# Sums over later keys in stick-breaking attention: one full-precision product and a running block replaced by two products of operand parts, with the steps of attention placed anew

## The chip, the cores and the metric

The kernel runs on one core of a Trainium2 chip. The metric is the device time of one execution in microseconds (us). Five engines matter: TensorE (PE in the profile; its weight loads are PEld), VectorE (DVE), ScalarE (ACT), GpSimd (POOL), and SyncE (SP), which issues most DMAs. Each runs its own queue of instructions in order and waits on semaphores.

## What is computed

One decoder layer on 512 tokens of width 2048, all in float32. The part that the change touches is the attention, with 8 heads of 128:

```python
z = jnp.einsum('bhqd,bhkd->bhqk', qi, kf).astype(jnp.float32) * scale
strict = key_pos[None, :] < q_pos[:, None]
log_beta = jax.nn.log_sigmoid(z)
log_1m = jnp.where(strict, jax.nn.log_sigmoid(-z), jnp.zeros_like(z))
tail = lax.cumsum(log_1m, axis=3, reverse=True) - log_1m
w = jnp.where(strict, jnp.exp(log_beta + tail), jnp.zeros_like(z))
return jnp.einsum('bhqk,bhkd->bhqd', w.astype(vf.dtype), vf)
```

For each query, `tail` at a key is the sum of `log_1m` over the later keys. Around it stand the projections `u, v_sgu, q, k, v_att, g_a, g_b = h @ W_in`, a spatial gating, the merge with `w_up_a`, `w_up_b` and `w_o`, a SwiGLU block (`w_ffn_in`, `w_ffn_out`) and a gate with per-layer embeddings (`w_gate`, `w_ple`).

## The kernel before

Activations lie transposed: 128 features on the partitions and the 512 tokens along the free axis. All large products are made from operand parts: a float32 operand is rounded by ScalarE into a high part of type float32r (L266 for activations, L334 for weights) and VectorE subtracts that from the operand for the low part (L267, L331). Three products, high by high, high by low and low by high, are summed in PSUM (`mm3`, L271 to L273). Most of them run in Strassen's form, seven products of 256 columns for a pair of 256 by 256 blocks; some are plain, with 512 columns. `Pair` (L572) makes two 128-row output tiles at once; `Pair.mix` (L645) puts the seven products together on ScalarE and VectorE, in a tile `o` that is either a home given by the caller or one of the two 128 by 1024 tiles of the pool tag `out` (`wide`).

Weights arrive through four landing buffers. SP loads them (L314, L316, L318), POOL issues a DMA that adds one block of the weights onto another as it lands (L338), ScalarE and VectorE split them into one of three slots. The order of the work is made in Python: `tick` counts units of the large products, and what has been put off with `after` or `beside` is written at its tick, between two units. A step that yields `n` goes on `n` ticks later. In the stage here a tick is one unit, 21 products of 256 columns.

The input projection goes in four rounds. A round makes q, k and v of two heads (one `Pair` each) and then three or four gate tiles; the attention of these two heads runs beside the following pairs (loop at L1195, order at L1124). Its steps, before the change:

- `q_prep` (L970) normalises q in place in the block `y_b[rnd]`, which is also q's home; `k_prep`, `v_prep` likewise. `flip` (L942, products at L946) transposes through PSUM.
- `stage_a` (L1002): one product of keys and queries in float32 (L1007) into a small PSUM bank (pool of two, also used by `flip`), four passes of ScalarE (L1009 to L1014), two of VectorE (L1016, L1018: `w`, the log of beta, and `zs`, minus `log_1m`) and POOL's mask of the diagonal block (L1020).
- `stage_b` (L1025): the sums over later keys. `tri` by `zs` in float32 (L1030) sums within the block of 128 keys, `ones` by `later` (L1032) adds the later blocks. `later` holds the sum of the later blocks' `zs`, kept by POOL (L1040) and VectorE (L1042). Then VectorE subtracts (L1034), ScalarE takes the exponential (L1044) and POOL masks (L1045).
- `finish` (L1050): four float32 products with v (L1054), a copy (L1056), and for the second head the store to DRAM (L1058).

A head has four key blocks, j = 3 to 0, with 128, 256, 384 and 512 query columns. The attention begins 5 ticks after v is made.

All of SBUF's working memory is two arenas, `parts` (float32r) and `wholes` (float32), in which blocks are taken and given while the program is written; `place` asks for a start at a multiple of `PLACE`. The size of the arenas and the places taken decide which earlier reader a DMA must wait for. `fits` decides at which tick an operand is built.

Of the kernel before, what the change touches and what calls it, by code (L numbers as in the profile page):

```python
# [12 lines left out]
F32 = mybir.dt.float32  # L13
F32R = mybir.dt.float32r
AF = mybir.ActivationFunctionType
ALU = mybir.AluOpType
# [21 lines left out]
PARTS = 16 * PLACE  # L38
WHOLES = 13824
# [26 lines left out]
def hybrid_layer(  # L66
# [44 lines left out]
    class Arena:  # L111
# [5 lines left out]
        def take(self, n, how="low"):  # L117
# [359 lines left out]
    def load(src, n=1024):  # L477
        b = take(n, "old")
        nc.sync.dma_start(out=b.f(0, 1024), in_=src)
        return b  # L480
# [91 lines left out]
    class Pair:  # L572
# [72 lines left out]
        def mix(self, o):  # L645
# [3 lines left out]
            s = tmp.tile([P, T], F32, tag="p75", name=nm("p75"), bufs=1)  # L649
            s7, s5 = s[:, :256], s[:, 256:]  # L650
# [24 lines left out]
        def mix_doubled(self, o):  # L675
# [4 lines left out]
            s5 = tmp.tile([P, T], F32, tag="p75", name=nm("p75"), bufs=1)[:, :256]  # L680
# [140 lines left out]
    def load_x():  # L821
# [109 lines left out]
    def a_tiles():  # L931

        for tag, n in (("l", T), ("later", 3 * P), ("w0", T), ("w1", 3 * P), ("w2", 2 * P), ("w3", P),
                       ("k", 1024), ("v", 1024), ("zs", 1024)):
            att[tag] = take(n)

# [33 lines left out]
    def q_prep(o):  # L970

        for h in range(2):
            yield 2
            s = o[:, h * T : (h + 1) * T]
            ps = flip(s)
# [7 lines left out]
            nc.scalar.activation(s, flip(q.f()), AF.Copy, scale=gcol[:, g_q : g_q + 1])  # L983
# [13 lines left out]
    def attention(rnd, qT, kT, rk, v):  # L997
        state = {}
        yield 1
        turn = [0]  # L1000

        def stage_a(h, j):  # L1002
# [5 lines left out]
            l = a_tile("l")[:, :n]  # L1008
            nc.scalar.activation(l, z, AF.Abs, scale=r)  # L1009
            turn[0] ^= 1  # L1010
            zs = a_tile("zs", n, turn[0] * T)
            nc.scalar.activation(zs, z, AF.Copy, scale=r)
            nc.scalar.activation(l, l, AF.Exp, scale=-1.0)
            nc.scalar.activation(l, l, AF.Ln, bias=1.0)  # L1014
            w = a_tile(f"w{j}", n)
            nc.vector.scalar_tensor_tensor(out=w, in0=zs, scalar=0.0, in1=l,  # L1016
                                           op0=ALU.min, op1=ALU.subtract)
            nc.vector.scalar_tensor_tensor(out=zs, in0=zs, scalar=0.0, in1=l,  # L1018
                                           op0=ALU.max, op1=ALU.add)
            nc.gpsimd.affine_select(out=zs[:, :P], in_=zs[:, :P], pattern=[[1, P]],  # L1020
                                    compare_op=ALU.is_gt, fill=0.0, base=0,
                                    channel_multiplier=-1)
            state[h, j] = zs, w

        def stage_b(h, j):  # L1025
# [4 lines left out]
            nc.tensor.matmul(tp, tri, sp, start=True, stop=j == NT - 1)  # L1030
            if j < NT - 1:
                nc.tensor.matmul(tp[:, P:], ones, later[:, j * P :], start=False,  # L1032
                                 stop=True)
            nc.vector.tensor_tensor(out=w, in0=w, in1=tp, op=ALU.subtract)  # L1034
            if j == NT - 1:
                later = a_tile("later", 3 * P)
                state[h, "later"] = later
            if j > 0:
                c = j * P
                nc.gpsimd.tensor_copy(later[:, c - P : c], sp[:, :P])  # L1040
# [21 lines left out]
        for h in range(2):  # L1062
            stage_a(h, 3)
            yield 2
            stage_a(h, 2)
            yield 1
            stage_b(h, 3)
            yield 1
            stage_a(h, 1)
            yield 1  # L1070
            stage_b(h, 2)
            yield 1
            stage_a(h, 0)
            yield 1
            stage_b(h, 1)
# [383 lines left out]
```

## Time and profile before

| what | us |
|---|---|
| time, median of 3 runs | 2718.68 |
| lowest and highest | 2717.98, 2721.21 |
| the profiled execution, its own time | 2719.95 |
| its span (first to last instruction) | 2718.3 |
| PE busy | 2693.0 |
| DVE busy | 2075.1 |
| ACT busy | 1353.5 |
| POOL busy | 449.2 |

Busy time of PE is modelled at the ends of instructions, so starts of neighbouring products say more than durations: the distance from one start to the next is what a product costs in a full queue. [...]

### The profile page before, as it was taken

The numbers are of one execution on the slowest core, as the hardware profiler recorded it, in microseconds if no ns is written. First come the engines' busy times: TensorE is split into PE (matmuls) and PEld (weight loads), VectorE is DVE, ScalarE is ACT, GpSimd is POOL, SyncE is SP. The second block draws the span as 40 slices with busy tenths as digits, with TensorE's granted clock in tenths as the row PEclk, the third lists the DMA queues.
The fourth block names the chain that finished last, engine by engine and source line by source line (L and its number), as shares of the span: only waits on it lengthen the run. The fifth ranks groups of instructions, "written<-read, shape, count | busy, mean of one in ns | idle before, by whom it ended". The sixth has DMA issues, their size and how long they took to land.

```text
span 2718.3 us, 45582 instructions
## 1 busy us (share of the span) xinstructions
PE 2693.0 (99%) x17243; PEld 2438.9 (90%) x17243; DVE 2075.1 (76%) x3377; ACT 1353.5 (50%) x2045; POOL 449.2 (17%) x527
## 2 busy tenths in 40 slices
PE   9999999999999999999999999999999999999999
PEld 7899999999999889988888888888888999989898
DVE  8566767667777667678889898989899567788876
ACT  7645556565554334365444444444445344453543
POOL 0222322232320000001111111111111111111110
PEclk9999999999999999999999999999999999999999
DMA  7567676767776447768888888887877669778784
GB/s 227 153 180 176 170 175 172 176 175 185 173 193 195 140 138 227 201 192 200 219 208 203 201 205 201 203 203 202 204 196 225 174 168 258 197 242 239 240 232 117
DMA packets 303132, 529.03 MB, mean 195 GB/s; under 512 B 25664, under 2 KB 162880, under 8 KB 302912
## 3 DMA queue, kind: packets, MB, share of 16 engines
q1 hardware_dynamic: 242160, 425.70, 49.0%
q0 software_dynamic: 60752, 100.43, 23.6%
q8 instruction: 135, 2.21, 0.3%
q14 instruction: 85, 0.70, 0.1%
HBM read 478.84 MB, written 47.19 MB: 194 GB/s over the span
## 4 chain that ended last, share of the span: by engine, by line
PE 95%; DMA 2%; DVE 1%; ACT 1%; issue 1%; POOL 0%; SPq 0%; ACTq 0%; DVEq 0%; POOLq 0%
PE ps L628 26%; PE ps L272 20%; PE ps L271 20%; PE ps L273 20%; PE small L628 4%; PE small L1054 1%; PE small L946 1%; PE small L1030 1%; PE small L1007 1%; DMA wholes<-x 0%; PE small L1032 0%; DMA ple<-out 0%; DVE wlo L331 0%; ACT whi L334 0%; PE small L1108 0%
## 5 line engine op out<-in xcount | busy, mean ns | idle before, releaser
L271 PE MATMUL ps<-parts,whi 128*128 128x256 f32 (+1 forms) x3995 | 1247.1, 314 | 13.3 <-ACT parts L266 7.4
L334 ACT ACTIVATE whi<-wholes 128x512 fp32r<-128x512 f32 (+4 forms) x950 | 856.1, 917 | 793.6 <-PE ps L272 305.3
L272 PE MATMUL ps<-parts,whi 128*128 128x256 f32 (+1 forms) x3960 | 1231.9, 311 | 1.3 <-DVE parts L267 1.3
L273 PE MATMUL ps<-parts,wlo 128*128 128x256 f32 (+1 forms) x3960 | 1230.4, 311 | 0.3 <-DVE wlo L331 0.3
L331 DVE TENSOR_TENSOR wlo<-wholes,whi 128x512 fp32r<-128x512 f32 (+4 forms) x950 | 964.9, 1050 | 156.5 <-ACT whi L334 155.0
L271 PEld LDWEIGHTS ps<-parts,whi 128*128 128x128 f32 x3995 | 764.2, 191 | 62.1 <-ACT parts L266 7.6
L272 PEld LDWEIGHTS ps<-parts,whi 128*128 128x128 f32 x3960 | 758.0, 191 | 44.7 <-DVE parts L267 2.2
L273 PEld LDWEIGHTS ps<-parts,wlo 128*128 128x128 f32 x3960 | 757.6, 191 | 38.9 <-DVE wlo L331 0.8
L628 PE MATMUL ps<-parts,whi 128*128 128x512 f32 x2064 | 683.2, 396 | 0.0
L628 PEld LDWEIGHTS ps<-parts,wlo 128*128 128x128 f32 x2064 | 387.9, 188 | 89.6
L628 PE MATMUL ps<-parts,wlo 128*128 128x256 f32 x2064 | 406.4, 278 | 0.0
L350 DVE TENSOR_TENSOR wholes<-wholes 128x256 f32<-128x256 f32 (+1 forms) x794 | 329.6, 415 | 27.5 <-issue 4.3
L628 PEld LDWEIGHTS ps<-parts,whi 128*128 128x128 f32 x2064 | 330.0, 189 | 2.1
L338 POOL DMA_DIRECT2D wholes<-w_ffn_in x172 | 149.7, 870 | 688.9 <-DVE wholes L350 229.7
L338 POOL DMA_DIRECT2D wholes<-w_in x132 | 118.8, 903 | 510.4 <-DMA wholes<-w_in 222.5
L687 DVE TENSOR_TENSOR out<-out,ps 128x256 f32<-128x256 f32 x258 | 107.6, 417 | 83.1 <-ACT out L684 83.0
L656 DVE TENSOR_TENSOR out<-out 128x256 f32<-128x256 f32 x59 | 25.0, 425 | 173.1 <-ACT out L653 172.8
L628 PE MATMUL small<-parts,whi 128*128 128x512 f32 x344 | 136.6, 397 | 0.0
L267 DVE TENSOR_TENSOR parts<-wholes,parts 128x1024 fp32r<-128x1024 f32 (+4 forms) x131 | 123.7, 953 | 14.0 <-ACT parts L266 13.5
L266 ACT ACTIVATE parts<-wholes 128x1024 fp32r<-128x1024 f32 (+4 forms) x131 | 105.7, 834 | 39.6 <-DVE wholes L497 15.6
L338 POOL DMA_DIRECT2D wholes<-w_ffn_out x56 | 57.0, 1031 | 401.0 <-DMA wholes<-w_ffn_out 187.5
L1299 ACT ACTIVATE out<-out 128x512 f32<-128x512 f32 x44 | 27.8, 633 | 161.2 <-DVE out L1298 161.2
(119 smaller groups left out, 1645.1 us busy)
## 6 DMA issues: line engine op xcount, KB each, us to landing
wholes<-w_ffn_in SPq DMA_DIRECT2D x172, 384.0 KB, 5.4
wholes<-w_in SPq DMA_DIRECT2D x132, 384.0 KB, 4.7
wholes<-w_ffn_in SPq DMA_DIRECT2D x172, 256.0 KB, 4.7
wholes<-w_ffn_in POOLq DMA_DIRECT2D x172, 256.0 KB, 5.2
wholes<-w_in SPq DMA_DIRECT2D x132, 256.0 KB, 3.8
wholes<-w_in POOLq DMA_DIRECT2D x132, 256.0 KB, 4.8
wholes<-x SPq DMA_DIRECT2D x32, 512.0 KB, 5.6
wholes<-w_ffn_out SPq DMA_DIRECT2D x31, 512.0 KB, 4.5
```

What stands on the lines that cost most here:

```text
L266: return (nc.scalar.activation(hi, src, AF.Copy), nc.vector.tensor_tensor(out=lo, in0=src, in1=hi.bitcast(F32), op=ALU.subtract))
L267: nc.vector.tensor_tensor(out=lo, in0=src, in1=hi.bitcast(F32), op=ALU.subtract))
L271: nc.tensor.matmul(ps[:, s], sh, mh[:, s], start=start, stop=False)
L272: nc.tensor.matmul(ps, sh, ml, start=False, stop=False)
L273: return nc.tensor.matmul(ps, sl, mh, start=False, stop=stop)
L331: in_turn(nc.vector.tensor_tensor(out=self.lo[:, blocks], in0=r, in1=h.bitcast(F32), op=ALU.subtract))
L334: in_turn(nc.scalar.activation(h, r, AF.Copy))
L338: nc.gpsimd.dma_start(out=raw[:, 3:5], in_=self.src[:, 1:3], accum_op=ALU.add)
L350: in_turn(nc.vector.tensor_tensor(out=o, in0=x, in1=y, op=ALU.add))
L628: m = nc.tensor.matmul(out, l, r, start=first and k == 0, stop=last and k == 1)
L687: in_turn(nc.vector.tensor_tensor(out=out, in0=x, in1=y, op=op))
L1299: nc.scalar.activation(g, g, AF.Silu)
```

## The change

The sum over later keys becomes two products of operand parts with one stationary matrix. `stage_b` now copies `zs` on ScalarE into its high part `zh`, `stage_c` makes the low part `zl` on VectorE, and `stage_d` multiplies `tri` by both in float32r. What the later blocks add comes in through row 0 of the operand: row 0 of a block's `zs` is not used by the sum within the block, so `tris[1]` has ones in row 0, and row 0 of the next block's `zs` is set to the sum of all keys of the later blocks (row 0 of the product plus the saved row 0, `first`). The running block `later`, its copies and additions, and the product with `ones` go. The former `stage_a` is cut in two: `stage_m` holds its VectorE and POOL part. The attention begins 6 ticks after k, with v made beside it, and a block takes three ticks.

Besides: q is made in an `out` tile and `y_b` is taken when q's first half is ready; `mix` works within `o` with three additions of 256 columns where it had one of 256 and one of 512; the arena `parts` grows by 1024 columns (for `zh` and `zl`) and `wholes` shrinks by 512; `place` starts at multiples of twice `PLACE`; the loads of the gate tiles take the lowest free place.

```diff
-PARTS = 16 * PLACE
-WHOLES = 13824
+PARTS = 16 * PLACE + 1024
+WHOLES = 13312
...
-                    start = -(-start // PLACE) * PLACE
+                    start = -(-start // (2 * PLACE)) * 2 * PLACE
...
-            copy(s, "q")
-            tt(b[:, 2], b[:, 1], s7)
-            tt(b[:, 1:4:2], b[:, 1:3], s5.unsqueeze(1).to_broadcast([P, 2, 256]))
+            copy(o[:, T:], "q")
+            tt(b[:, 2], b[:, 1], b[:, 2])
+            tt(b[:, 1], b[:, 1], b[:, 3])
+            tt(b[:, 3], b[:, 2], b[:, 3])
...
-    tri = consts.tile([P, P], F32, name="tri")
+    tris = [consts.tile([P, P], F32R, name=f"tri{i}") for i in range(2)]
+    tri = tmp.tile([P, P], F32, tag="diag", name="tri")
     nc.gpsimd.affine_select(out=tri, in_=ones, pattern=[[-1, P]], compare_op=ALU.is_gt,
                             fill=0.0, base=0, channel_multiplier=1)
+    nc.vector.tensor_copy(tris[0], tri)
+    nc.vector.memset(tri[0:1, :], 1.0)
+    nc.vector.tensor_copy(tris[1], tri)
...
+        def stage_m(h, j):
...
+            if j < NT - 1:
+                if j:
+                    nc.gpsimd.tensor_copy(first(j), s[0:1])
+                nc.gpsimd.memset(s[0:1, :P], 0.0)
+
+        def stage_b(j):
+            nc.scalar.activation(zh[:, : (NT - j) * P], sums(j), AF.Copy)
+
+        def stage_c(j):
             n = (NT - j) * P
-            sp, w = state.pop((h, j))
-            later = state.get((h, "later"))
-            tp = small_bank()[:, :n]
-            nc.tensor.matmul(tp, tri, sp, start=True, stop=j == NT - 1)
-            if j < NT - 1:
-                nc.tensor.matmul(tp[:, P:], ones, later[:, j * P :], start=False,
-                                 stop=True)
+            in_turn(nc.vector.tensor_tensor(out=zl[:, :n], in0=sums(j), in1=att["zh"].f(0, n),
+                                            op=ALU.subtract))
+
+        def stage_d(h, j):
+            n, w = (NT - j) * P, weights(h, j)
+            tp, t = small_bank()[:, :n], tris[j < NT - 1]
+            nc.tensor.matmul(tp, t, zh[:, :n], start=True, stop=False)
+            nc.tensor.matmul(tp, t, zl[:, :n], start=False, stop=True)
+            if j:
+                nc.vector.tensor_tensor(out=sums(j - 1)[0:1, P:], in0=tp[0:1], in1=first(j),
+                                        op=ALU.add)
             nc.vector.tensor_tensor(out=w, in0=w, in1=tp, op=ALU.subtract)
-            if j == NT - 1:
-                later = a_tile("later", 3 * P)
-                state[h, "later"] = later
-            if j > 0:
-                c = j * P
-                nc.gpsimd.tensor_copy(later[:, c - P : c], sp[:, :P])
-                if j < NT - 1:
-                    nc.vector.tensor_tensor(out=later[:, c:], in0=later[:, c:], in1=sp[:, P:],
-                                            op=ALU.add)
             nc.scalar.activation(w, w, AF.Exp)
...
+        blocks = [(h, j) for h in range(2) for j in range(NT - 1, -1, -1)]
+        stage_a(*blocks[0])
+        yield 1
+        stage_m(*blocks[0])
+        yield 1
+        stage_a(*blocks[1])
+        for i, (h, j) in enumerate(blocks):
+            ahead = blocks[i + 1 : i + 3]
+            stage_b(j)
             yield 1
+            if i == NT:
+                finish(0)
+            stage_c(j)
+            if ahead:
+                stage_m(*ahead[0])
             yield 1
+            stage_d(h, j)
+            if ahead[1:]:
+                stage_a(*ahead[1])
             yield 1
+        yield 1
+        finish(1)
...
         elif w == "k":
             kT, rk = o, rms_tile()
             beside(k_prep(kT, rk))
+            beside(attention(i, kT, rk, a_tile("v", 1024)), 6)
         elif w == "v":
-            v = a_tile("v", 1024)
-            beside(v_prep(o, v))
-            beside(attention(i, qT, kT, rk, v), 5)
+            beside(v_prep(o, a_tile("v", 1024)))
...
-            s = load(gate_spill[b, j], PLACE if b == "a" and OUT[j] == "S" else 1024)
+            s = load(gate_spill[b, j], PLACE if b == "a" and OUT[j] == "S" else 1024,
+                     "low")
```

More of the change, by code (lines that the diff above doesn't have):

```diff
@@ L475, in cut, with load @@
         return x.rearrange("p (b c) -> p b c", c=256)
-    def load(src, n=1024):
-        b = take(n, "old")
+    def load(src, n=1024, how="old"):
+        b = take(n, how)
         nc.sync.dma_start(out=b.f(0, 1024), in_=src)
@@ L931, in a_tiles @@
     def a_tiles():
-        for tag, n in (("l", T), ("later", 3 * P), ("w0", T), ("w1", 3 * P), ("w2", 2 * P), ("w3", P),
-                       ("k", 1024), ("v", 1024), ("zs", 1024)):
+        for tag, n in (("l", T), ("w0", T), ("w1", 3 * P), ("w2", 2 * P), ("w3", 2 * P),
+                       ("first", 5 * P), ("k", 1024), ("v", 1024), ("zs", 1024)):
             att[tag] = take(n)
+        for tag in ("zh", "zl"):
+            att[tag] = parts.take(T, "high")
     def a_tile(tag, n=T, start=0):
@@ L982, in q_prep @@
             yield 2
-            nc.scalar.activation(s, flip(q.f()), AF.Copy, scale=gcol[:, g_q : g_q + 1])
+            if not h:
+                y_b[i] = take(1024)
+            nc.scalar.activation(y_b[i].f(h * T, (h + 1) * T), flip(q.f()), AF.Copy,
+                                 scale=gcol[:, g_q : g_q + 1])
             give(q)
@@ L995, in v_prep, with attention, sums, weights @@
             times(v[:, h * T : (h + 1) * T], flip(o[:, h * T : (h + 1) * T]), norm1.cols)
-    def attention(rnd, qT, kT, rk, v):
+    def attention(rnd, kT, rk, v):
         state = {}
         yield 1
-        turn = [0]
+        qT = y_b[rnd].f()
+        zh, zl = (att[t].own() for t in ("zh", "zl"))
+        def sums(j):
+            return a_tile("zs", (NT - j) * P, j % 2 * T)
+        def weights(h, j):
+            return a_tile(f"w{j}", (NT - j) * P, (j == NT - 1) * h * P)
+        def first(j):
+            return (sums(j) if j == NT - 1 else a_tile("first", (NT - j) * P, (j == 1) * 2 * P))[0:1]
         def stage_a(h, j):
@@ L1130, in block @@
     def block(w, i):
-        if w == "q":
-            y_b[i] = take(1024)
-            return y_b[i].f()
         if w == "k":
```

46 lines of the change are left out of this document (11 added, 35 removed).

## Prediction

> **What bounds the kernel.** I read the page first (busy shares, then the chain that ended last), then the busy time by stretches, then what PE waited for (total, times, longest). Beside them lies the order in which the changed program gives each engine its instructions (below: the order); it holds no times.
>
> ```profile
> span 2718.3 us, 45582 instructions
> PE 2693.0 (99%) x17243; PEld 2438.9 (90%) x17243; DVE 2075.1 (76%) x3377; ACT 1353.5 (50%) x2045; POOL 449.2 (17%) x527
> PE 95%; DMA 2%; DVE 1%; ACT 1%; issue 1%; POOL 0%; SPq 0%; ACTq 0%; DVEq 0%; POOLq 0%
> ```
> ```profile
> core 0: us, PE busy (x) PEld busy (x) DVE busy (x) ACT busy (x) POOL busy (x), PEclk, DMA share, GB/s
> ...
> 185.00:260.00 75.00, 75.00 (x628) 74.81 (x627) 51.39 (x83) 41.61 (x81) 16.84 (x18) 1.00 0.71 177
> 260.00:350.00 90.00, 89.57 (x679) 83.91 (x679) 60.14 (x101) 50.21 (x86) 26.59 (x37) 1.00 0.71 179
> ```
> ```profile
> PE ps L271 <- ACT parts L266: 7.4, 2, 4.9
> PE small L946 <- ACT wholes L968: 2.2, 1, 2.2
> ...
> PE small L1054 <- POOL wholes L1045: 1.7, 4, 0.4
> PE ps L272 <- DVE parts L267: 1.3, 1, 1.3
> ```
>
> PE is the bound everywhere: 95% of the chain, and in a round with attention (260 to 350) it idles 0.43 of 90 us, while DVE is busy 67%, ACT 56%, the DMA engines 71%, at the full granted clock of 1.00. So PE time that goes is time that goes, until another engine is full. The attention itself hardly waits: its one entry is L1054, four times. What a product costs is read from the distance of starts in a full queue.
>
> ```profile
> 129.68 0.28 PE L273 MATMUL ps<-parts,wlo 128*128 128x256 f32 x1
> 129.80 0.81 PE L1030 MATMUL small<-wholes,tri 128*128 128x384 f32 x2
> 130.45 0.59 PE L1032 MATMUL small<-wholes,ones 128*128 128x256 f32 x2
> 130.69 0.47 PE L271 MATMUL ps<-parts,whi 128*128 128x256 f32 x1
> 131.00 0.28 PE L272 MATMUL ps<-parts,whi 128*128 128x256 f32 x1
> ```
> ```profile
> 1000.09 0.39 PE L272 MATMUL ps<-parts,whi 128*128 128x512 f32 x1
> 1000.32 0.39 PE L273 MATMUL ps<-parts,wlo 128*128 128x512 f32 x1
> ```
> ```profile
> 246.06 0.60 PE L946 MATMUL small<-ident,wholes 128*128 128x128 f32 x4
> ...
> 246.62 0.28 PE L272 MATMUL ps<-parts,whi 128*128 128x256 f32 x1
> ```
>
> A float32r product of 256 columns starts 0.12 after the one before (129.68 to 129.80), one of 512 columns 0.23 (1000.09 to 1000.32; 0.227 over longer runs). The float32 pair at 129.80 and the L271 behind it take 1.20 up to 131.00; less 0.12 that is 1.08 us for 384 + 256 columns, 1.69 ns a column, almost four times float32r's 0.44. Four float32 transposes take 0.44 (246.06 to 246.62, less 0.12), 0.11 each.
>
> **The change, part by part.**
>
> *The products.* Before, a head puts 1280 columns through `tri` (128 + 256 + 384 + 512) and 768 through `ones`: 2048 x 8 heads x 1.69 ns = 27.7 us. After, each block has two float32r products: 0.12 for 128 columns (the 256-column row; none this narrow stands in the trace), 0.12, 0.173 (the middle of 256 and 512) and 0.227, so 2 x 0.64 = 1.28 us a head, 10.2 in all. That takes off 17.4 us (27.65 - 10.24). Bounds for the 128-column ones: half the 256-column row, 0.06, or the float32 rate, 128 x 1.69 = 0.217; sixteen of them make the term -18.4 to -15.8.
>
> *The wait of the first `finish`.*
>
> ```profile
> 142.33 0.28 PE L273 MATMUL ps<-parts,wlo 128*128 128x256 f32 x1
> 143.04 2.20 PE L1054 MATMUL small<-wholes 128*128 128x512 f32 x6 [0.43 <-POOL wholes L1045]
> ```
> ```profile
> L1045 POOL TENSOR_SCALAR_AFFINE_SELECT wholes<-wholes x32: 292/695/1952, 122.4 to 621.3; 128x128 f32<-128x128 f32 x32
> L1040 POOL COPY wholes<-wholes x24: 289/394/2217, 113.7 to 608.1; 128x128 f32<-128x128 f32 x24
> ```
>
> L1054 starts 0.71 after its predecessor where 0.12 is the queue's own pace: 0.59, in four rounds 2.4 us. In the changed order the first finish stands 43 to 44 products behind the last one that its mask rests on, where it stood 33 behind with a DMA wait of POOL between; that wait goes. The second finish now stands 33 behind (4.0 us), without the DMA, for a subtraction, an exponential and a mask of up to 1.95. I put back a quarter: -1.8, bounds -2.4 and 0.
>
> *A new wait for a small bank.* v's transposes now fall among the attention steps, and both draw on the two small banks. In rounds 1 to 3 the third score product (L1027, 384 columns) comes ten instructions behind v's four transposes and needs the bank that four scalings still read.
>
> ```profile
> L968 ACT ACTIVATE wholes<-small,cols 128x128 f32<-128x128 f32 x32 | 9.4, 372 | 13.9 <-PE small L946 13.9
> L946 PE MATMUL small<-ident,out 128*128 128x128 f32 x28 | 4.7, 293 | 0.0
> ```
>
> From the start of the last transpose ACT needs 0.29 + 4 x 0.372 = 1.78; PE has that transpose, two narrow products and seven of 256, 0.11 + 9 x 0.12 = 1.19. It waits 0.59, three times: +1.8 (0 if ACT starts on the first transpose, 4 if ACT is 0.7 late each time). Behind L1027 stands the whole PE queue. The next such product has twenty in between, 2.4 us, and is covered.
>
> *The chain of a block.* Product, row sum (DVE), high part (ACT), low part (DVE), next products: three ticks, 63 products, 7.6 us.
>
> ```profile
> L331 DVE TENSOR_TENSOR wlo<-wholes,whi 128x512 fp32r<-128x512 f32 x92 | 64.4, 700 | 0.0
> L331 DVE TENSOR_TENSOR wlo<-wholes,whi 128x1280 fp32r<-128x1280 f32 x92 | 138.5, 1505 | 52.9 <-ACT whi L334 52.5
> L334 ACT ACTIVATE whi<-wholes 128x512 fp32r<-128x512 f32 x91 | 56.9, 625 | 24.2 <-DVE wholes L350 24.0
> L1034 DVE TENSOR_TENSOR wholes<-wholes,small 128x512 f32<-128x512 f32 x8 | 5.5, 686 | 2.1 <-PE small L1032 2.1
> ```
>
> With the widest rows it is 0.69 + 0.63 + 0.70 = 2.0 us, and behind one large split on DVE at each of its two turns (1.5 each) 5.0: covered, cost 0. The row sum (one partition) and POOL's one-row copy and memset are not in the trace. I take a full-width op of the same columns, 0.69 for DVE and 0.4 for POOL (the middle of L1040); ends 0 and 0.69, 0 and 2.2. They lie beside PE too. DVE gains 32 low parts (0.49 in the mean, as 0.70 for 512 columns scales), 24 row sums, loses 16 additions: some 6 us a round on 60 of 90. ACT gains 4 on 50. Both still fit.
>
> *`mix`* gives DVE three additions of 256 for one of 256 and one of 512.
>
> ```profile
> L656 DVE TENSOR_TENSOR out<-out 128x256 f32<-128x256 f32 x17 | 7.2, 425 | 45.5 <-ACT out L653 45.2
> L656 DVE TENSOR_TENSOR out<-out,p 128x512 f32<-128x512 f32 x17 | 11.7, 691 | 0.4
> ```
>
> That is 1.28 for 1.12, 0.16 a pair, at DVE's 67%: 0; uncovered, 69 pairs would make 11 us (as a bound on the other side, -0 since no PE wait on L656 is listed). q in an `out` tile, the later `y_b` and its moved SP store, and the gate loads' places are covered by the same PE work; the order shows no new wait of PE near them: 0.
>
> *The start.* The two `tri` tiles add three short ops to DVE, and SP's order changes: the third `w_first` load was issued behind the second store and now stands behind the third, with a 512 KB load of x ahead.
>
> ```profile
> 14.42 1.22 SPq L314 DMA_DIRECT2D wholes<-w_first  x2
> 16.93 0.33 SPq L808 DMA_DIRECT2D ple<-out  x1
> ```
> ```profile
> 24.47 0.51 PE L271 MATMUL ps<-parts,whi 128*128 128x512 f32 x1 [0.25 <-ACT whi L334]
> 26.46 0.50 PE L271 MATMUL ps<-parts,whi 128*128 128x512 f32 x1 [0.78 <-ACT whi L334]
> ```
>
> It goes out some 2 us later (17.3 against 15.6 at the latest), and PE already waits for weights at 24.47 and 26.46, so part of this reaches PE: +1.5, bounds 0 and 4.
>
> *Stage boundaries.* The arenas' sizes and places reorder the loads between stages. The 1.3 us wait on L267 listed above no longer has its place in the changed order; in the last stage a new product stands right behind a large weight split (L334). I take 0, bounds -5 and 5, about the sum of the waits listed there (7.4 less the 4.9 at the start, 1.3, and as much again).
>
> **Sum**: -17.4 - 1.8 + 1.8 + 1.5 + 0 = -15.9 on the profiled execution's 2719.95 gives 2704.05. That execution lay 1.27 above the median of the three runs, so **2702.8** against 2718.68.
>
> [...] L1045 and L1040 are the same small operations each time and took from 0.29 to 2.2 us. [...]
>
> **Rivals.**
>
> 1. *POOL's row work comes late, and it is slower.* POOL also issues the adding DMAs and stops there for landings.
>
> ```profile
> L338 POOL DMA_DIRECT2D wholes<-w_in x132 | 118.8, 903 | 510.4 <-DMA wholes<-w_in 222.5 <-DVE wholes L350 92.5 <-DVE wlo L331 62.3
> ```
> ```profile
> 301.49 0.90 POOL L338 DMA_DIRECT2D wholes<-w_in  x1 [5.72 <-DVE out L656]
> ```
>
> In seven of the eight heads the order has row copy, L338, then the memset for the block of 384 columns, and both new products wait for that memset. A wait like the one at 301.49, 5.7, issuing 0.9, a memset as slow as the slowest copy, 2.2, high and low part 1.3: 10.1. The order leaves 44 products, 5.3 us, in a first head and 67, 8.0 us, in a second. So 4.8 late three times and 2.1 four times, 22.8 us, with nothing to cover it on PE: 2719.95 - 15.9 + 22.8 - 1.27 = 2725.6. It decides from 2.3 us late in the mean (15.9 / 7). For it: POOL idles 510 us ahead of L338. Against: the mask L1020 stood in the same queue ahead of L1030, and PE's list has no wait on it. [...]
> 2. *The narrow types gain less than said.* If float32r products of a moving operand that was just split ran at the transposes' 0.84 ns a column (0.11 for 128), 20480 columns cost 17.2 instead of 10.2: 2709.8. Against: the rows at 0.44 to 0.47.
> 3. *The start, the banks and the boundaries take their upper bounds in part*: 10 more, 2713. For it: PE waits there already.
> 4. *They fall out well*: 10 less, 2693.
>
> **How the numbers follow.** Forecast 0.72, rival 1 0.05, rival 2 0.06, rival 3 0.12, rival 4 0.05. All terms at their lower bounds give -25.8 (2692.9), at their upper ones -2.8 (2715.9); 2695 to 2712 leaves out rival 1, about half of rival 3 and rival 4, and the ends of the forecast. No change is within 0.2%, 5.4 us, about what a measurement of this kernel can tell: 2713.2 to 2724.1. Faster: the forecast, rivals 2 and 4 and half of 3, 0.89; same: the other half, 0.06; slower: rival 1, 0.05.
>
> **What would show it.** Right: 64 records of float32r products on `tri`, one each, 0.12 to 0.23 apart from the next start; L1032's gone; PE still 99% busy; pairs of units in a round with attention closer together. The bank: L1027 with an idle gap of about 0.6 behind L974, three times. Wrong: PE waiting on ACT's L1051 or DVE's L1055 (the chain is late), with POOL's L1048 behind an L338; records of the narrow products 0.2 apart; or new waits ahead of 40 us or around 2070, 2400 and 2550.

## The result

| | before | after |
|---|---|---|
| time, median of 7 runs each, us | 2721.21 | 2711.6 |
| lowest and highest, us | 2715.9, 2728.2 | 2707.1, 2712.72 |
| profiled execution: span, us | 2718.3 | 2709.9 |
| ratio of times (95% interval) | | 0.9961 (0.9948 to 0.9975) |

Faster by 0.39%, about 10 us. In the profiled executions the span is shorter by 8.35 us (2718.25 to 2709.90), and these two are compared below. The forecast was 15.9 less. Its direction was right; by the two profiled executions half of its size is missing, by the times about a third (9.6 us by the medians, 10.6 by the ratio). 2711.6 lies just inside the upper end of the range that was given, 2695 to 2712.

The page of after, the rows that answer to those of before (PE's share of the chain of work that ended last fell from 95 to 93%):

```profile
span 2709.9 us, 45610 instructions
PE 2678.2 (99%) x17195; PEld 2427.8 (90%) x17195; DVE 2098.2 (77%) x3489; ACT 1364.7 (50%) x2077; POOL 448.6 (17%) x543
PE 93%; DVE 2%; DMA 2%; ACT 1%; issue 1%; POOL 0%; SPq 0%; ACTq 0%; DVEq 0%; POOLq 0%
```

To see where the time went, cut the span at two products that stand in every version: the first of those that spread column sums out (L860 before, L864 after) and the first of the spatial gating (L1108, L1134). All attention lies between. Their starts, then busy times between these starts (PE first), before and after:

```profile
L860 PE MATMUL small<-diag,ones x24: 270/275/377, 76.3 to 2566.5; 128*128 128x128 f32 x24
L1108 PE MATMUL small<-wholes x64: 273/275/377, 668.5 to 792.8; 128*128 128x128 f32 x64
```
```profile
76.30:668.50 592.20, 588.07 (x4576) 562.61 (x4575) 402.33 (x670) 339.24 (x646) 158.33 (x207) 1.00 0.70 175
```
```profile
L864 PE MATMUL small<-diag,ones x24: 270/273/377, 78.6 to 2554.1; 128*128 128x128 f32 x24
L1134 PE MATMUL small<-wholes x64: 272/275/276, 661.2 to 785.0; 128*128 128x128 f32 x64
```
```profile
78.60:661.20 582.60, 574.44 (x4527) 555.38 (x4526) 419.53 (x734) 351.09 (x678) 160.86 (x223) 0.99 0.72 178
```

The start lost 2.3 us (76.3 to 78.6), the stretch with the attention won 9.6 (592.2 to 582.6), all that follows won 1.1. In the stretch PE's busy time fell by 13.6, but its idle time doubled, from 4.1 to 8.2: the products did become cheaper, and new waits took part of it back. What PE waited for in after (total, times, longest):

```profile
PE ps L271 <- ACT parts L266: 9.0, 4, 4.7
...
PE small L952 <- ACT wholes L974: 2.5, 1, 2.5
PE small L1062 <- DVE parts L1055: 2.3, 4, 1.8
PE small L1027 <- ACT wholes L974: 1.9, 3, 0.6
...
PE small L1027 <- ACT wholes L991: 0.7, 1, 0.7
...
PE small L1077 <- POOL wholes L1068: 0.5, 1, 0.5
```

The four waits of the first finish (L1054 before) are gone. L1062 (the second product, waiting for the low part) and L1027 (the score product, waiting for a bank) are new. The list understates both: it counts only the idle gap. The longest, as PE and as VectorE saw it:

```profile
142.75 0.28 PE L273 MATMUL ps<-parts,wlo 128*128 128x256 f32 x1
142.87 0.34 PE L1061 MATMUL small<-parts,tri 128*128 128x384 f32 x1
145.05 0.44 PE L1062 MATMUL small<-parts,tri 128*128 128x384 f32 x1 [1.84 <-DVE parts L1055]
```
```profile
139.72 0.42 DVE L654 TENSOR_TENSOR out<-out 128x256 f32<-128x256 f32 x1 [2.06 <-ACT out L651]
140.06 2.09 DVE L331 TENSOR_TENSOR wlo<-wholes,whi 128x1280 fp32r<-128x1280 f32 x2
142.06 1.34 DVE L654 TENSOR_TENSOR out<-out 128x256 f32<-128x256 f32 x3
143.50 0.42 DVE L654 TENSOR_TENSOR out<-out,ps 128x256 f32<-128x256 f32 x1
143.84 0.68 DVE L654 TENSOR_TENSOR out<-ps,out 128x512 f32<-128x512 f32 x1
144.44 0.55 DVE L1055 TENSOR_TENSOR parts<-wholes,parts 128x384 fp32r<-128x384 f32 x1
```

PE reached the pair of products at 142.87 and could start the second 2.18 later, where 0.17 is the queue's pace. The low part (L1055) took 0.55, but it stood in VectorE's queue behind two weight splits (L331) and the additions that end a pair (L654), and the first of these had kept VectorE idle for 2.06 until ScalarE had made a copy for it (L651). The same place costs the products of 384 columns only 0.16 in the other three rounds. What round 0 had besides begins at POOL and reaches VectorE further back:

```profile
135.82 0.89 POOL L338 DMA_DIRECT2D wholes<-w_in  x1 [1.17 <-DMA wholes<-w_in]
136.38 0.49 POOL L1047 COPY wholes<-wholes 1x384 f32<-1x384 f32 x1
```
```profile
136.91 0.41 DVE L1064 TENSOR_TENSOR wholes<-small,wholes 1x256 f32<-1x256 f32 x1 [2.39 <-POOL wholes L1047]
```

POOL stood at an adding DMA (L338) until a load of w_in had landed, and its one-row copy (L1047) came behind it. VectorE's row sum (L1064) waited 2.39 for that copy, the subtraction L1066 came next, ScalarE's exponential (L1067) waited 1.78 for the subtraction, and L651 stood behind it in ScalarE's queue. From the start of the pair of 256 columns (L1061 at 133.87) to the start of L1055 it took 10.57 us here, and 8.64 in each of the other three rounds. So the place behind the end of a pair used up the slack, and POOL's late copy added 1.9. The clock makes it dearer; granted clock is the column after POOL's:

```profile
145.05:146.50 1.45, 1.45 (x11) 1.45 (x12) 1.45 (x4) 0.14 (x1) 0.88 (x1) 0.98 0.83 335
146.50:149.80 3.30, 3.30 (x18) 3.30 (x17) 3.30 (x6) 2.58 (x5) 0.60 (x2) 0.50 0.81 161
```

1.5 us after the wait the clock is granted at half for 3.3 us: products of 256 columns start 0.21 apart instead of 0.12, sixteen of them, which costs another 1.5 us.

**Theory** for the experiments: the gain of the products is all there, and about 10 us of it are given back by waits that can be removed. **Rivals**: the engines beside PE are full, so that a removed wait comes back at the next instruction; or the products themselves are dearer in place.

### The profile page after: what moved, and what is told of

Its sections match the earlier page's. It is cut to its first block, busy times and chain, and to the rows that moved or that the text cites. A ratio compares the mean times of both kernels' runs of the same rounds, so it can differ in the third digit from the quotient of the medians.

```text
span 2709.9 us, 45610 instructions
## 1 busy us (share of the span) xinstructions
PE 2678.2 (99%) x17195; PEld 2427.8 (90%) x17195; DVE 2098.2 (77%) x3489; ACT 1364.7 (50%) x2077; POOL 448.6 (17%) x543
## 4 chain that ended last, share of the span: by engine, by line
PE 93%; DVE 2%; DMA 2%; ACT 1%; issue 1%; POOL 0%; SPq 0%; ACTq 0%; DVEq 0%; POOLq 0%
PE ps L628 27%; PE ps L272 20%; PE ps L273 20%; PE ps L271 20%; PE small L628 4%; PE small L1077 1%; PE small L1027 1%; PE small L952 1%; DVE wlo L331 1%; ACT whi L334 0%; DMA wholes<-x 0%; DMA wholes<-w_in 0%; DVE parts L267 0%; DVE out L654 0%; PE small L1134 0%
## 5 line engine op out<-in xcount | busy, mean ns | idle before, releaser
L334 ACT ACTIVATE whi<-wholes 128x512 fp32r<-128x512 f32 (+4 forms) x950 | 858.1, 917 | 834.6 <-PE ps L272 301.5
L331 DVE TENSOR_TENSOR wlo<-wholes,whi 128x512 fp32r<-128x512 f32 (+4 forms) x950 | 963.7, 1048 | 119.0 <-ACT whi L334 118.4
L338 POOL DMA_DIRECT2D wholes<-w_ffn_in x172 | 149.8, 871 | 693.9 <-DVE wholes L350 228.5
L654 DVE TENSOR_TENSOR out<-out 128x256 f32<-128x256 f32 x248 | 104.9, 423 | 173.2 <-ACT out L651 169.0
L338 POOL DMA_DIRECT2D wholes<-w_in x132 | 117.5, 892 | 516.4 <-DMA wholes<-w_in 184.0
L266 ACT ACTIVATE parts<-wholes 128x1024 fp32r<-128x1024 f32 (+4 forms) x131 | 105.7, 834 | 42.0 <-DVE wholes L497 19.6
L338 POOL DMA_DIRECT2D wholes<-w_ffn_out x56 | 56.9, 1019 | 399.4 <-DMA wholes<-w_ffn_out 164.2
```

The lines of the kernel that those rows point to most:

```text
L266: return (nc.scalar.activation(hi, src, AF.Copy), nc.vector.tensor_tensor(out=lo, in0=src, in1=hi.bitcast(F32), op=ALU.subtract))
L331: in_turn(nc.vector.tensor_tensor(out=self.lo[:, blocks], in0=r, in1=h.bitcast(F32), op=ALU.subtract))
L334: in_turn(nc.scalar.activation(h, r, AF.Copy))
L338: nc.gpsimd.dma_start(out=raw[:, 3:5], in_=self.src[:, 1:3], accum_op=ALU.add)
L654: in_turn(nc.vector.tensor_tensor(out=out, in0=x, in1=y, op=op))
```

## The experiments

Each is an edit of the kernel after unless it says otherwise. "The stretch" is the time between the two starts above (592.2 before, 582.6 after), read from the same two lines of each profile. The kernel before, run beside them, had medians of 2720.76, 2721.39 and 2723.47 in the three sets.

### Two ticks from the low part to the products

```diff
                 stage_m(*ahead[0])
-            yield 1
+            yield 2
             stage_d(h, j)
```

> The changed kernel with one more tick between a block's low part and its two products. Theory (the gain of the products is all there; about 10 us of it were given back by new waits, and a removed wait comes off the time): the waits of L1062 on L1055 go (2.0 us in round 0 with 1.5 us of half clock behind it, and 1.25 us in the four second heads), and the third score product no longer stands behind v's transposes (3 x 0.8 us): 7 us less than the changed kernel, ratio to before about 0.9935 where the changed kernel has 0.9961; PE lists no wait on L1055. Rival (the engines beside PE are full in these rounds, so a removed wait comes back at the next instruction): within 2 us of the changed kernel, ratio 0.9955 to 0.9965, with new PE waits on L1064, L1066 or L1068.

2702.6 us, ratio 0.9933 (0.991 to 0.9956). The stretch took 571.7 us, 10.9 less than in after. PE between the same starts (77.3 and 649.0), and two of the rows of its list:

```profile
77.30:649.00 571.70, 568.68 (x4527) 551.87 (x4526) 416.19 (x734) 353.95 (x678) 165.70 (x223) 1.00 0.71 181
```
```profile
PE small L952 <- ACT wholes L974: 2.4, 1, 2.4
...
PE small L1077 <- POOL wholes L1068: 0.5, 1, 0.5
```

As many products as in after (x4527), 5.8 us less busy and 5.1 less idle; no entry of L1062 or L1027 is left in the list. The theory holds: by the ratios of the two kernels it is 7.6 us less than after, where 7 was expected. It wasn't the engines: VectorE's work is the same 416 us in a shorter stretch. And the sum closes: 592.2 - 571.7 = 20.5, of which 17.1 are the products (27.7 before, 10.6 now, from the first start of each group to the second large product behind it, less 0.12), 2.4 the first finish, and about 0.8 a stretch of half clock that before had behind a wait at 100 us and this run hadn't. The edit moves all later steps of the attention too: VectorE's row sum no longer waits for POOL's copy, and the third score product no longer meets v's transposes. So the run takes away the chain's waits and the bank's together, and doesn't tell how much is owed to each.

### v's transposes a tick later

```diff
         for h in range(2):
-            yield 2
+            yield 3 - 2 * h
             times(v[:, h * T : (h + 1) * T], flip(o[:, h * T : (h + 1) * T]), norm1.cols)
```

> The changed kernel with v's transposes one tick later for the first head of v, the second head directly behind; nothing else moved. Theory: the three waits of the third score product on v's scalings (L1027 on L974, 0.8 us each) go, the one of round 0 (0.9 us) and the waits on L1055 stay: 2.4 us less, ratio to before about 0.9952. Rival: v's own transposes now wait for a bank that the attention holds, and it comes to nothing: ratio 0.996, PE waiting at L952 on L1066 or L1030.

2713.53 us, ratio 0.9967 (0.9956 to 0.9977): no gain, and the rival is right. L1027's entry on v's scalings is gone, and in its place stands

```profile
PE small L952 <- DVE wholes L1066: 2.4, 3, 0.8
```

With two small banks, whoever comes third waits: the first transposes now take the bank of the block's products, which the subtraction L1066 still reads. The stretch is 2.3 us shorter in this profile, since the second finish's waits (0.9) and part of the half clock are missing too; the times show nothing of it.

### Without the low part

```diff
-            in_turn(nc.vector.tensor_tensor(out=zl[:, :n], in0=sums(j), in1=att["zh"].f(0, n),
-                                            op=ALU.subtract))
+            return
...
-            nc.tensor.matmul(tp, t, zh[:, :n], start=True, stop=False)
-            nc.tensor.matmul(tp, t, zl[:, :n], start=False, stop=True)
+            nc.tensor.matmul(tp, t, zh[:, :n], start=True, stop=True)
```

> The changed kernel without the low part: the subtraction L1055 and its product are left out, so the sums rest on the high part alone. Theory: the second of the two products goes (0.11 + 0.12 + 0.175 + 0.23 = 0.64 us for each of 8 heads, 5.1 us) and with it all waits on L1055 (4.7 us with the half clock): 9.8 us less than the changed kernel, ratio about 0.9925. Rival: the chain of a block is late already in its high part or in POOL's row copy, so a wait on ACT's L1051 takes the place: 5.1 us less, ratio 0.9942.

2699.56 us, ratio 0.9922 (0.9898 to 0.9946). The stretch is 13.9 us shorter than in after: 5.3 for the 32 products, the rest waits and the half clock behind them (none between its two starts). No wait on L1051 took the place (two finishes waited for a mask, 1.5 us in all), so of the operands of the two products only the low part came too late for PE. It also shows what the parts cost when they are placed well: e1_two_ticks, with them, is 3 us longer.

### Float32 products on the row of later sums

```diff
-            nc.tensor.matmul(tp, t, zh[:, :n], start=True, stop=False)
-            nc.tensor.matmul(tp, t, zl[:, :n], start=False, stop=True)
+            nc.tensor.matmul(tp, t, sums(j), start=True, stop=True)
```

(`stage_b` and `stage_c` do nothing, `tris` is float32.)

> The changed kernel with its row of later sums kept, but one float32 product a block instead of two float32r products of parts; no high and low parts at all. By the trace of before a float32 product costs 0.224, 0.432, 0.646 and 0.859 us at the four widths, 17.3 us for 8 heads, against 10.6 us now: 6.7 us more. Theory: the waits on L1055 (4.7 us) go with the parts, so 2 us more than the changed kernel, ratio about 0.9968: the row of later sums brings most of the gain, the parts little. Rival (the waits come back at the row sum, or never cost anything): 6.7 us more, ratio 0.9986.

2710.35 us, ratio 0.9955 (0.9939 to 0.9971), and the stretch is 577.7 us: 4.9 shorter than in after, although its products cost 17.3 us in place of 10.6. Neither side expected that. But the profiled execution, 2705.66, is the fastest of the five; by the ratios (0.9955 and 0.9961, with overlapping intervals) the two kernels can't be told apart. With the parts go the waits on L1055, the half clock behind one of them, and also most of the waits of the bank, probably since ScalarE has no high part to make ahead of v's scalings. Of the attention only L952 (2.0) and L1027 on L991 (0.2) are left in PE's list. So of the change as made, the row of later sums (2048 columns become 1280) and the new order brought the gain, and the parts, as placed, won nothing that the times show.

### x loaded to the lowest free place

```diff
-        x_raw.append(take(1024, "old"))
+        x_raw.append(take(1024))
```

> e1_two_ticks with one thing more: x is loaded to the lowest free place instead of the one free longest, which puts the second and third load of w_first ahead of the first store of the start again (in the changed kernel the third goes out at 17.8 us, before at 14.4). Theory (the late loads cost the start 0.6 to 2.3 us, by the traces of the changed kernel and of four kernels with the same start): the first 76 us end as early as before or up to 1 us earlier, 1 to 2 us less than e1_two_ticks, ratio to before about 0.9928. Rival (the start waits for the bytes, not for the order in which they are asked for): the first 76 us are unchanged or later, since x now comes behind the weights.

2706.34 us, ratio 0.9939 (0.9925 to 0.9953). The first column product starts at 77.1, against 77.3 in e1_two_ticks: the rival is right, the order of the loads isn't what holds the start. The wait at 21.3 went, and others of 1.7 and 1.3 us came at 15.1 and 42.3. The stretch took 573.8, 2.1 more than in e1_two_ticks: about 1.0 behind the wait at 101 us, where the clock was granted at half for 3.4 us and in e1_two_ticks was not, and about 1 at the second finishes. Its program is the same there but for the places of buffers.

### The new additions alone

The kernel before, with `mix` as in the diff of the change.

> The kernel before with the new order of additions at the end of a pair (three additions of 256 columns in place of one of 256 and one of 512) and nothing else. Theory (VectorE has room beside PE wherever a pair ends): no difference, within 2 us of before, ratio 0.9995 to 1.0005, no new PE wait. Rival (each end of a pair is uncovered by 0.16 us): 69 pairs, 11 us more, ratio 1.004.

2721.38 us, ratio 1.0002 (0.9992 to 1.0011), and PE's list has no new wait on an addition: nothing, as the theory said.

### The memory plan alone

The kernel before, with that `mix`, the sizes of the arenas, `place` and the gate loads of the change; the attention is that of before.

> The kernel before with the new mix and with the memory plan of the changed kernel (sizes of the two arenas, places in steps of 3584 columns, gate loads at the lowest place); attention as before. Theory: this alone makes the late start (0.6 to 2.3 us in the first 76 us) and the new product behind a large split in the last stage (L334, 1.3 us); the attention keeps its time. In all 1 to 4 us more than before, ratio 1.0005 to 1.0015. Rival (the start is late because of the two tri tiles): the first 76 us as before.

2725.58 us, ratio 1.0018 (1.0008 to 1.0027): 5 us lost. The first column product is 1.2 us late, without any change in `tri`; the stretch takes 591.0. The greater part is behind 2000 us. PE's first rows from there on, of this kernel and of before:

```profile
PE ps L271 <- ACT parts L266: 7.4, 3, 4.6
PE ps L271 <- ACT whi L334: 1.9, 2, 1.1
```
```profile
PE ps L271 <- ACT parts L266: 2.5, 1, 2.5
...
PE ps L271 <- ACT whi L334: 0.7, 1, 0.7
```

Operands of the last stages come later. Over the eleven kernels here with the new plan, L266's entry from 2000 us on runs from 2.6 to 7.4 us (4.3 in after); with the old plan it is 2.3 to 2.5 in three of three. Why just these operands are late (which reader their places wait for) stays open. Its ten runs also had a lower granted clock than the 21 of before beside them, 0.9972 against 0.9982 in the mean; if PE is the bound, that is an estimated 2.7 of the 5 us.

### The attention one tick later

`beside(attention(...), 7)` for 6. A pair has eight ticks and a block three, so another block's low part falls on the ticks at a pair's end.

> The changed kernel with its attention begun one tick later (7 for 6). A pair has eight ticks and a block three; so each head's low parts fall on another tick of a pair. Theory (PE waits on L1055 where a low part stands in VectorE's queue behind the additions of a pair's end, and on L1027 where v's transposes share its tick): no wait of the third score product on L974 any more (2.4 us), and the waits on L1055 move: none at the 384 columns of a first head, but at the 512 columns of the second heads (last tick of a pair), 0.3 to 2 us each, and perhaps at their 128 columns. Time 2707 to 2714. Rival (the widest low parts are late by their own length): the waits stay where they were, at 384 in round 0 and at 512 with 0.3.

One run, 2717.87 us (before: 2721.39), above the expected 2714. The waits moved as the theory said:

```profile
PE small L1062 <- DVE parts L1055: 3.7, 5, 1.2
PE small L1077 <- POOL wholes L1068: 2.8, 5, 1.9
```

L1027 waits for L974 no more; L1062 waits at the 512 columns of all four second heads (0.4 to 1.4 us beyond its pace), and none of it is at 384 columns of a first head. One at 384 of a second head (0.6) wasn't expected, and neither were the finish's. The stretch took 583.2, 0.6 more than in after; most of the excess lies behind it, where the clock was granted at half four times, and once in after.

### The extra tick behind the products

```diff
                 stage_a(*ahead[1])
-            yield 1
-        yield 1
+            yield 2
         finish(1)
```

> The changed kernel with the extra tick of e1_two_ticks put elsewhere: behind a block's products, not ahead of them. A block takes four ticks as there, so its low parts stand on the third and seventh tick of a pair and never behind the additions of its end (the last two), but the products still come one tick behind the low part, and the third score product shares a tick with v's transposes. Theory (the place in VectorE's queue made the wait): no wait on L1055, the three waits of L1027 on L974 (0.8 us each) stay: attention 7 to 9 us shorter than in the changed kernel. Rival (one tick is too short for high part, low part and what is queued ahead of them): waits on L1055 stay, now at the same ticks of every pair, and the attention is no shorter.

One run, 2721.64 us (before: 2723.47); the stretch took 587.6, 4.9 more than in after, and the rest of the 10 us more came behind it, where the clock was granted at half four times. The theory is right on L1055, of which no wait is left with the same single tick, and wrong on the sum:

```profile
PE small L1077 <- POOL wholes L1068: 7.4, 4, 2.4
...
PE small L1027 <- ACT wholes L974: 2.0, 3, 0.7
```

The last block's subtraction (L1066) now falls on a pair's end, behind its additions. But that isn't what the second finish waits for:

```profile
485.90 0.68 DVE L1066 TENSOR_TENSOR wholes<-wholes,small 128x512 f32<-128x512 f32 x1
```
```profile
489.69 0.86 POOL L338 DMA_DIRECT2D wholes<-w_in  x1 [6.71 <-ACT whi L334]
490.24 0.70 POOL L1068 TENSOR_SCALAR_AFFINE_SELECT wholes<-wholes 128x128 f32<-128x128 f32 x1
```

The exponential runs from 486.62 to 487.25, and its mask (L1068) stands in POOL's queue behind an adding DMA (L338) that is held until 489.69. It is so in all four rounds: the mask follows L338 at once, 1.4 to 3.0 us after its exponential had ended. Behind two of these waits of the finish (2.1 and 2.4) the clock is granted at half for 3.4 us. So without that place there is no wait on L1055, and POOL's queue took the gain back.

### Two ticks, on the worst ticks

e1_two_ticks with `beside(attention(...), 8)`: every low part of 256 and 512 columns stands on the last tick of a pair.

> e1_two_ticks with the attention begun two ticks later (8 for 6): every low part of 256 and 512 columns now stands on the last tick of a pair, behind its additions, with two ticks to its products. Theory in its strict form (only the place counts): waits on L1055 at the 512 columns, 0.3 to 1.4 us each as in e8_tick_7, up to 8 of them, 3 to 8 us more than e1_two_ticks. Rival (two ticks cover the queue in any place): no wait on L1055, the attention as short as in e1_two_ticks.

One run, 2708.51 us (before: 2723.47); no wait on L1055. The rival is right on the wait: two ticks cover the queue in this place too. The attention isn't as short: the stretch took 575.7, 4.0 more than in e1_two_ticks; v's transposes now meet their own scalings in the banks (L952 on L974: 3 waits, 3.6 us, one of them also in e1_two_ticks with 2.4).

### Float32 products with the old memory plan

e4_f32 with the arena sizes, `place` and gate loads of before, since without parts nothing needs the new ones.

> e4_f32 (one float32 product a block on the row of later sums, no parts) with the memory plan of the kernel before: without parts, the 1024 columns for them in the arena of parts and what went with them (arena sizes, places, gate loads) aren't needed. Theory (that plan costs about 5 us, by e7_plan's ratio of 1.0018): 5 us less than e4_f32, ratio about 0.9937, the first 76 us and the last stages as before. Rival (e7_plan's cost came with its old attention): as e4_f32, 0.9955.

2706.6 us, ratio 0.9939 (0.9924 to 0.9953), against 0.9955 for e4_f32: 4 us less, about as the theory said, though the two intervals overlap. The start is that of before (76.2) and so is L266's entry from 2000 us on, 2.3. The stretch is 2.4 us longer than in e4_f32; 1.8 of it arises between 102 and 106 us, where the clock was granted at half here and in full there.

### Two ticks, and one more ahead of the second finish

```diff
             yield 1
-        yield 1
+        yield 2
         finish(1)
```

(on e1_two_ticks)

> e1_two_ticks with one more tick ahead of the second finish. Theory: its wait on POOL's mask (0.6 us in one round there, 0.9 in two rounds of the changed kernel) goes, and nothing else moves: 0.6 us less than e1_two_ticks, ratio about 0.993. Rival (the finish then meets the next round's q): no gain, or up to 2 us more.

2702.42 us, ratio 0.9922 (0.9909 to 0.9935): the lowest ratio of the versions that compute the whole sum, though its interval takes in e1_two_ticks. The finish's wait is gone, as the theory said; the stretch is 571.7 as in e1_two_ticks, so the 0.6 us can't be told from the rest.

## Why the prediction was half right

The terms of its sum, against the profile of after:

| step | predicted | measured | from |
|---|---|---|---|
| products | -17.4 | -17.1 | 27.7 to 10.6, by distances of starts |
| finish | -1.8 | -1.4 | first: -2.4; second: 0.3 and 0.7 beyond its pace |
| small bank | +1.8 | +3.0 | 3 x 0.8 and 0.9 beyond its pace, less 0.3 that before had |
| chain of a block | 0 | +5.2 | see below |
| start | +1.5 | +2.3 | 76.3 to 78.6 |
| the rest of the stretch | 0 | +0.7 | what is left of -9.6 |
| after the stretch | 0 | -1.1 | -7.25 at 661 us, -8.35 at the end |
| sum | -15.9 | -8.4 | |

**Products: right.** The 64 records are there, one each (before, the 32 float32 products of L1030 show as 64), and L1032's are gone. Two heads' rows of a narrow and of a wider pair:

```profile
302.30 0.28 PE L273 MATMUL ps<-parts,wlo 128*128 128x256 f32 x1
302.42 0.22 PE L1061 MATMUL small<-parts,tri 128*128 128x128 f32 x1
302.48 0.28 PE L1062 MATMUL small<-parts,tri 128*128 128x128 f32 x1
302.60 0.86 PE L1027 MATMUL small<-wholes 128*128 128x384 f32 x2
```
```profile
319.37 0.28 PE L273 MATMUL ps<-parts,wlo 128*128 128x256 f32 x1
319.49 0.34 PE L1061 MATMUL small<-parts,tri 128*128 128x384 f32 x1
319.67 0.34 PE L1062 MATMUL small<-parts,tri 128*128 128x384 f32 x1
319.84 0.28 PE L271 MATMUL ps<-parts,whi 128*128 128x256 f32 x1
```

The first narrow one takes 0.06, the lower bound, and the second 0.12, where float32 follows; 384 columns take 0.18 and 0.17 against the 0.173 of the sum. Rival 2 is out (by the row that it rests on, 0.11 for 128 columns, its rate is 0.86 ns a column and not 0.84, which changes nothing).

**The chain of a block: the step that failed.** "Covered, cost 0" compared the time that the steps take, 5.0 us at the most, with the 7.6 us of three ticks. It let one large split stand ahead of each of VectorE's turns, and left out what else has its place in that queue: the additions at a pair's end. It also took POOL's row copy at 0.4 us beside PE's work, with nothing ahead of it. Measured: 2.0 at 384 columns in round 0, 1.5 of half clock behind it, 1.2 in the second heads (three times 0.32 and 0.22), 0.5 in three pairs of 384 columns that came 0.16 late each.

The place in VectorE's queue made the last two, 1.7, and 0.16 of round 0. Its sign stood in a row that the prediction quoted for its price alone: L656 with "45.5 <-ACT out L653", 2.7 us of idle VectorE ahead of each of 17 additions. In the second head of round 1 L651 itself waits for PE's own last products (0.26 at 323.62).

The other 1.8 of round 0, and with it the half clock, came by way of POOL's copy behind an L338. That is the mechanism of rival 1, at a step that it didn't name. It reckoned with the memset in seven of the eight heads, where the order is copy, L338, memset; in the eighth, the first head of round 0, L338 stands ahead of the copy. The memset was not it: PE's list has no wait that leads to an L338 ahead of L1048. Nor did the 22.8 us come that rival 1 would have cost. In e2_v_later the same order gave the same wait: VectorE stood 2.18 for the copy, and the second product came 1.7 late. No run moves the copy alone, so this share is read from these two traces and not tested.

PE waiting on L1055 was one of the prediction's own signs of being wrong, and it came. Two ticks of slack (e1_two_ticks, e10_two_ticks_8) take the wait away, and so does another place (e9_gap_behind), although there VectorE waits for POOL's copy seven times, 5.9 us in all. The chain stood in the sum at 0 and without bounds; that the time still fell inside the range is owed to the width given to the start, the bank and the boundaries.

In the rows at 139.72 to 144.44 VectorE kept the order of its queue: L1055's high part had been ready since 141.6 (L1051, from 141.09, took 0.53), and L1055 began at 144.44, behind the additions.

**The small bank: right place, too small.** The gap of 0.6 was there three times, but a waiting float32 product starts 0.8 late by its neighbours' starts (266.08 to 267.01, less 0.12), and round 0 had one more (0.9, on L991), since there q, k and v end together.

**The start: right in size, not in its reason.** 2.3 in this profile; the nine kernels here with the same order of loads lie at 0.6 to 2.3 behind before, 1.6 in the mean. In e7_plan the memory plan alone makes it 1.2. That it hangs on the order of w_first's loads, as the prediction had it, is not borne out: e5_two_ticks_x_low turned that order round and won nothing.

**The finish.** The first heads' wait went as said, by the order. The 32 new low parts on VectorE did not make POOL's masks longer in the mean: 946 ns before, 941 after, and 1129 where the low parts were left out (e3_no_low). The second finish was not "without the DMA": in all four rounds of after an L338 comes just ahead of its mask, and in two (333.21, 470.95) it makes the finish late.

```profile
L1045 POOL TENSOR_SCALAR_AFFINE_SELECT wholes<-wholes 128x128 f32<-128x128 f32 x32 | 30.3, 946 | 0.4
```
```profile
L1068 POOL TENSOR_SCALAR_AFFINE_SELECT wholes<-wholes 128x128 f32<-128x128 f32 x32 | 30.1, 941 | 9.0 <-ACT wholes L1067 9.0
```

**mix: right** (e6_mix_only). **Stage boundaries: 0 by luck.** Behind 2000 us PE's waits on L266 and L334 are 3.0 longer in after than in before (4.3 against 2.5, 1.9 against 0.7), as new places in memory could make them. What hid it is the clock: from 661 us on it was granted at half once in after (but for the last microseconds) and three times in before, for 3.4 us each. How often this happens differs between executions: the mean granted clock of the 21 runs of before beside e8_tick_7 was 0.997 to 0.999. With one such time, what follows the stretch took 2048.7 and 2048.9 us with the new plan (after, e4_f32) and 2046.8 with the old (e6_mix_only); with four, 2053.8 to 2054.8 (e2, e5, e8, e9). By itself the memory plan lost 5 us in e7_plan, the upper bound that the prediction gave.

## What to carry to other kernels

A chain through several engines that looks covered by its own durations (here 5.0 us at the most in ticks of 7.6) is covered only if the queues that it passes are clear at that tick: read the idle column of what stands ahead of it, and ask whether that work waits for the engine that is to be fed, or for an engine that stops for transfers, as POOL does here (in after it stood 184 us ahead of L338 for loads of w_in). Give such a chain slack in units of that queue's longest wait, here two ticks for one, which made 0.9933 of 0.9961 (part of it at the small banks). When an edit needs memory, price the new places of the buffers by a kernel that has them and nothing else.

## What the runs showed of the hardware that was not expected

- Waits of PE of about 2 us were mostly followed by half clock: 3.4 us at 0.50 in after behind the wait at 143, 1.5 us of cost. Not every one was: the wait of 2.2 to 2.5 us at about 101 us was followed by half clock in after and in before, and not in e1_two_ticks. In the fourteen profiles PE waited more than 1.8 us 17 times between 60 and 700 us. With 14 of these waits the clock was granted at half for 3.41 us, beginning 1.9 to 3.4 us after the wait began; with three (2.0 to 2.4 us) it was not, nor with any of the seven waits of 1.0 to 1.8 us.
- A VectorE addition of 384 columns on one partition took as long as on 128 (538 and 534 ns), and a one-row copy of 384 columns on POOL 1.1 us in the mean, where clearing 128 columns of that row took 0.24:

```profile
L1066 DVE TENSOR_TENSOR wholes<-wholes,small 128x384 f32<-128x384 f32 x8 | 4.3, 534 | 0.0
L1064 DVE TENSOR_TENSOR wholes<-small,wholes 1x384 f32<-1x384 f32 x8 | 4.3, 538 | 0.0
```
```profile
L1047 POOL COPY wholes<-wholes 1x384 f32<-1x384 f32 x8 | 8.9, 1108 | 0.4
L1048 POOL MEMSET wholes<- 1x128 f32 x24 | 5.7, 237 | 1.0
```
